# Batched x·yᵀ: stores of two heads in 16 KB runs with 64-column weight tiles, instead of four heads in 32 KB runs with 32-column tiles

## The chip, the cores and the metric

The kernel runs on one core of a Trainium2 chip. The metric is device time in microseconds, median of several executions. A trace of one core has a "span" from its first to its last instruction, here about 1.8 us shorter than the device time.

PE is the matrix engine and writes its results into a memory called PSUM; DVE and ACT copy them out of it, POOL casts inputs, and SP issues the DMAs. 16 DMA engines move the data, in packets; here a packet is one contiguous run of a partition (the 22 stores of before, 128 partitions each, are 2816 packets of 32 KB in the trace). PE gets a granted clock that varies: PEclk shows it in tenths of full speed, and "half clock" below is a 5 there (in the trace of before it is 1.00 up to 65 us, then mostly 0.50, and 0.634 in the mean). The page shows two queues of the kind "instruction"; one of their packets is called an "instruction fetch" below: 16 KB each on queue q8, 8 KB each on q14.

## The reference

```python
# x, y: (8, 12, 512, 64) float32; 96 heads of 512 rows
def reference(x, y):
    return np.einsum('bhtc,bhsc->bhts', x, y).astype(np.float32)
```

The inputs are 25 MB, the output is 101 MB. Each head is a 512 x 512 result with a contraction of 64.

## The kernel before

A group `g` is eight heads: `a` selects the half of the partitions that holds the contraction, and four heads lie beside each other in the columns. A partition of an output tile belongs to one head and holds 16 consecutive rows, 32 KB, which are contiguous in the output.

```python
P, G, Q, R, K = 128, 4, 32, 16, 8          # heads a tile, partitions a head, rows a partition, R/2
ov = out....rearrange("(g a p n) -> g a p n", a=2, p=P, n=R * S)
opool = tc.tile_pool(name="opool", bufs=3)  # output tiles of 32 KB a partition
# ... prepare(g): load, cast on POOL, transpose on PE, copy to xT and yT (half on DVE, half on ACT)
            dst = xT[:, half * K:(half + 1) * K]
            if half == 0:
                nc.vector.tensor_copy(dst, pt)
            else:
                nc.scalar.activation(dst, pt, COPY)
# ... main loop
        for a in range(2):
            ot = opool.tile([P, R, S], fp32)
            otf = ot.rearrange("p r s -> p (r s)")
            edge = (g == 0 and a == 0) or (g == NG - 1 and a == 1)
            for k in range(K):
                ...
                pm = pmpool.tile([P, 2, S], fp32)      # a PSUM tile
                for two in range(2):
                    for h in range(G):
                        nc.tensor.matmul(pm[h * Q:(h + 1) * Q, two, :],
                            xT[a * C:(a + 1) * C, 2 * k + two, h * Q:(h + 1) * Q],
                            yT[a * C:(a + 1) * C, h * S:(h + 1) * S], start=True, stop=True)
                # copy pm to ot[:, 2k:2k+2], on ACT for even k, on DVE for odd k
                if edge and k % 2 == 1:
                    i, j = (2 * k - 2) * S, (2 * k + 2) * S
                    nc.sync.dma_start(ov[g, a][:, i:j], otf[:, i:j])
            if not edge:
                nc.sync.dma_start(ov[g, a], otf)
```

Of the kernel before, what the change touches and what calls it, by code (L numbers as in the profile page):

```python
# [1 line left out]

# [5 lines left out]


@with_exitstack  # L10
def kernel(
    ctx: ExitStack,
    tc: tile.TileContext,
    x: bass.AP,
    y: bass.AP,
    out: bass.AP,
):





    nc = tc.nc
    B, H, T, C = x.shape
    _, _, S, _ = y.shape
    P = 128
    G = 4
    Q = P // G
    R = T // Q
    NG = B * H // (2 * G)  # L30
    K = R // 2
    AHEAD = 3
    fp32 = mybir.dt.float32
    bf16 = mybir.dt.bfloat16
    COPY = mybir.ActivationFunctionType.Copy
    assert C * 2 == P and S == T and R == 16

    xv = x.rearrange("b h t c -> (b h t c)").rearrange("(g a p n) -> g p a n", a=2, p=P, n=R * C)
    yv = y.rearrange("b h t c -> (b h t c)").rearrange("(g a p n) -> g p a n", a=2, p=P, n=R * C)
    ov = out.rearrange("b h t s -> (b h t s)").rearrange("(g a p n) -> g a p n", a=2, p=P, n=R * S)  # L40

    const = ctx.enter_context(tc.tile_pool(name="const", bufs=1))
    lpool = ctx.enter_context(tc.tile_pool(name="lpool", bufs=AHEAD))
    bpool = ctx.enter_context(tc.tile_pool(name="bpool", bufs=2))
    tpool = ctx.enter_context(tc.tile_pool(name="tpool", bufs=2))
    opool = ctx.enter_context(tc.tile_pool(name="opool", bufs=3))
    ptpool = ctx.enter_context(tc.tile_pool(name="ptpsum", bufs=2, space=bass.MemoryType.PSUM))
    pmpool = ctx.enter_context(tc.tile_pool(name="pmpsum", bufs=3, space=bass.MemoryType.PSUM))

    loaded = {}  # L50

    def load(g):
        xs = lpool.tile([P, 2, R, C], fp32)
        ys = lpool.tile([P, 2, R, C], fp32)
        nc.sync.dma_start(ys.rearrange("p a r c -> p a (r c)"), yv[g])  # L55
        nc.sync.dma_start(xs.rearrange("p a r c -> p a (r c)"), xv[g])
        loaded[g] = (xs, ys)

    for g in range(AHEAD):
        load(g)  # L60

    ident = const.tile([P, P], bf16)
    make_identity(nc, ident)

    def prepare(g, made):

        xs, ys = loaded.pop(g)
        yb = bpool.tile([P, R, 2, C], bf16)
        xb = bpool.tile([P, R, 2, C], bf16)
        for s, b in ((ys, yb), (xs, xb)):  # L70
            for half in range(2):
                rows = slice(half * K, (half + 1) * K)
                nc.gpsimd.tensor_copy(b[:, rows], s[:, :, rows].rearrange("p a r c -> p r a c"))  # L73
        if g + AHEAD < NG:
            load(g + AHEAD)
        yield
        yT = tpool.tile([P, G * Q, R], bf16)
        xT = tpool.tile([P, R, P], bf16)
        for half in range(2):
            pt = ptpool.tile([P, K, P], bf16)  # L80
            for k in range(K):
                nc.tensor.transpose(  # L82
                    pt[:, k, :], yb[:, half * K + k].rearrange("p a c -> p (a c)"), ident
                )
            dst = yT[:, :, half * K:(half + 1) * K]
            src = pt.rearrange("p k n -> p n k")
            if half == 0:
                nc.vector.tensor_copy(dst, src)  # L88
            else:
                nc.scalar.activation(dst, src, COPY)  # L90
            yield
        for half in range(2):
            pt = ptpool.tile([P, K, P], bf16)
            for k in range(K):
                nc.tensor.transpose(  # L95
                    pt[:, k, :], xb[:, half * K + k].rearrange("p a c -> p (a c)"), ident
                )
            dst = xT[:, half * K:(half + 1) * K]
            if half == 0:
                nc.vector.tensor_copy(dst, pt)  # L100
            else:
                nc.scalar.activation(dst, pt, COPY)  # L102
            yield
        made[g] = (xT, yT.rearrange("p n k -> p (n k)"))

    made = {}
    for _ in prepare(0, made):
        pass
    for g in range(NG):
        xT, yT = made.pop(g)  # L110
        steps = prepare(g + 1, made) if g + 1 < NG else iter(())
        for a in range(2):
            ot = opool.tile([P, R, S], fp32)
            otf = ot.rearrange("p r s -> p (r s)")
            edge = (g == 0 and a == 0) or (g == NG - 1 and a == 1)
            for k in range(K):
                if k in (0, 3, 6):
                    next(steps, None)
                pm = pmpool.tile([P, 2, S], fp32)
                for two in range(2):  # L120
                    for h in range(G):
                        nc.tensor.matmul(  # L122
                            pm[h * Q:(h + 1) * Q, two, :],
                            xT[a * C:(a + 1) * C, 2 * k + two, h * Q:(h + 1) * Q],
                            yT[a * C:(a + 1) * C, h * S:(h + 1) * S],
                            start=True, stop=True,
                        )
                if k % 2 == 0:
                    nc.scalar.activation(ot[:, 2 * k:2 * k + 2, :], pm, COPY)  # L129
                else:  # L130
                    nc.vector.tensor_copy(ot[:, 2 * k:2 * k + 2, :], pm)  # L131
                if edge and k % 2 == 1:
                    i, j = (2 * k - 2) * S, (2 * k + 2) * S
                    nc.sync.dma_start(ov[g, a][:, i:j], otf[:, i:j])
            if not edge:
                nc.sync.dma_start(ov[g, a], otf)  # L136


# [1 line left out]
_INS = ['x', 'y']  # L140
_OUTS = [((8, 12, 512, 512), 'float32')]


# [23 lines left out]
```

## Time and profile before

| | before |
|---|---|
| median time | 307.29 us (307.26 to 307.49) |
| span of the trace | 305.6 us |
| DMA data queue, share of 16 engines | 97.2% |
| PE, DVE, ACT busy | 67%, 45%, 39% |
| matmuls in all (with transposes) | 1920 |

The page of the kernel before. The slices are fortieths of the span, a digit is a busy share in tenths; the queue lines give packets, MB and share of 16 engines.

```profile
PE 203.8 (67%) x1920; PEld 91.5 (30%) x1920; DVE 138.4 (45%) x120; ACT 119.6 (39%) x121; POOL 49.3 (16%) x54
...
PEclk9999999975555555755675555575575555555555
DMA  7999999999999999999999999999999999999980
...
q1 hardware_dynamic: 10848, 125.83, 97.2%
q8 instruction: 15, 0.25, 0.3%
q14 instruction: 4, 0.03, 0.0%
...
L122 PE MATMUL pm<-yT,xT 64*32 64x512 bf16 x1536 | 159.4, 586 | 67.2 <-ACT ot L129 64.7
...
L100 DVE COPY xT<-pt 128x1024 bf16<-128x1024 bf16 x12 | 8.3, 690 | 12.3 <-PE pt L95 9.8
...
out_dram<-ot SPq DMA_DIRECT2D x22, 4096.0 KB, 27.4
```

DMA is at 9 from the second to the last but one busy slice: this kernel is bound by data movement (97.2% of 16 engines' span), and the compute engines wait for it (ACT 72.1 us and DVE 63.4 us for stores that still hold the output buffers). Then only two things can change the time by much: how long a DMA engine needs for its share, and how unevenly the 16 engines finish.

The trace also holds single packets and, for each DMA, the times of its 16 completions (one per DMA engine, as I read them: before each of the 16 of the last store a data packet ends, 0.43 us before it at most). In the packed trace a packet carries no engine number, but on an engine one packet begins where the one before it ends (within 20 ns in the chains followed), so an engine that is apart from the others can be followed. Sorted completions of the last store, as the distance behind the first of them:

```
kernel before, last store (us): first engine done at 295.86; then
+0.01 +0.18 +0.22 +0.71 +0.90 +0.93 +1.63 +2.60 +2.75 +2.82 +3.16 +3.28 +3.72 +4.66 +8.79
```

The other 15 engines have done their share by about 300.5 us, and the core waits four more microseconds for a single DMA engine. That one engine sets the end. Below it is called the drifting engine, because its lag grows from store to store.

The pace of the matmuls at half clock is read from an unbroken stretch in the timeline of before (start us, us, engine, line and what). 64 matmuls are eight PSUM tiles, so a tile takes 6.82 / 8 = 0.853 us. Within it, four matmuls start within 30 ns of each other, and the next four about 0.43 us after them: four run abreast.

```profile
266.39 6.82 PE L122 MATMUL pm<-yT,xT 64*32 64x512 bf16 x64 [3.19 <-ACT ot L129]
```

### The profile page before, as it was taken

To read this page: it belongs to the slowest core of one execution; us is meant where nothing else is said; L and a number is where in the kernel's file an instruction comes from. 1 tells how busy PE (TensorE), PEld (TensorE's weight loads), DVE (VectorE), ACT (ScalarE), POOL (GpSimd) and SP (SyncE) were. 2 spreads that over 40 slices of the span, in tenths; PEclk is the share of its full clock that TensorE was granted. 3 is DMA by queue.
4 is the path that set the end of the run, shared out by engine and by line. 5 is a ranking of instruction groups with operands and counts; after the bars stand their busy time and mean duration, and the time that the engine had idled before them with its cause. 6 is when DMAs were issued, how large, how long until landed. Compare 5 with 4: busy or idle time off the path is not lost.

```text
span 305.6 us, 4378 instructions
## 1 busy us (share of the span) xinstructions
PE 203.8 (67%) x1920; PEld 91.5 (30%) x1920; DVE 138.4 (45%) x120; ACT 119.6 (39%) x121; POOL 49.3 (16%) x54
## 2 busy tenths in 40 slices
PE   1899999969919928936932990991785976575000
PEld 1443234525404503512511540350251432222000
DVE  0465654657416507615633741670664664446000
ACT  1445527544523606505522451560653463325000
POOL 3755024300500500320140050041000000000000
PEclk9999999975555555755675555575575555555555
DMA  7999999999999999999999999999999999999980
GB/s 278 412 409 420 459 419 399 470 418 388 446 455 388 440 446 398 441 429 437 427 424 442 420 427 430 411 454 420 437 435 425 427 442 422 437 437 422 409 368 39
DMA packets 10867, 126.11 MB, mean 413 GB/s; under 512 B 864, under 2 KB 864, under 8 KB 7008
## 3 DMA queue, kind: packets, MB, share of 16 engines
q1 hardware_dynamic: 10848, 125.83, 97.2%
q8 instruction: 15, 0.25, 0.3%
q14 instruction: 4, 0.03, 0.0%
HBM read 25.17 MB, written 100.66 MB: 412 GB/s over the span
## 4 chain that ended last, share of the span: by engine, by line
DMA 49%; PE 29%; DVE 5%; issue 4%; ACT 3%; POOL 1%; SPq 0%; ACTq 0%
DMA out_dram<-ot 47%; PE pm L122 23%; DVE ot L131 5%; PE pt L95 4%; ACT ot L129 3%; PE pt L82 2%; DMA xs<-in_x_dram 2%; ACT xT L102 1%; POOL xb L73 1%; DVE xT L100 0%; SPq L55 0%; ACTq L129 0%; SPq L136 0%
## 5 line engine op out<-in xcount | busy, mean ns | idle before, releaser
L122 PE MATMUL pm<-yT,xT 64*32 64x512 bf16 x1536 | 159.4, 586 | 67.2 <-ACT ot L129 64.7
L131 DVE COPY ot<-pm 128x1024 f32<-128x1024 f32 x96 | 117.0, 1224 | 123.0 <-DMA out_dram<-ot 63.4
L129 ACT ACTIVATE ot<-pm 128x1024 f32<-128x1024 f32 x96 | 95.9, 1023 | 115.5 <-DMA out_dram<-ot 72.1
L122 PEld LDWEIGHTS <-xT 64*32 64x32 bf16 x1536 | 53.3, 118 | 148.1 <-issue 136.3
L73 POOL CAST yb<-ys 128x1024 bf16<-128x1024 f32 x24 | 24.3, 1040 | 143.5 <-PE pt L82 69.8
L82 PE MATMUL pt<-ident,yb 128*128 128x128 bf16 x192 | 23.9, 297 | 8.5 <-POOL yb L73 6.8
L102 ACT ACTIVATE xT<-pt 128x1024 bf16<-128x1024 bf16 x12 | 12.3, 1023 | 37.0 <-PE pt L95 30.3
L95 PE MATMUL pt<-ident,xb 128*128 128x128 bf16 x192 | 25.8, 310 | 1.3 <-DVE xT L100 0.8
L73 POOL CAST xb<-xs 128x1024 bf16<-128x1024 f32 x24 | 24.3, 1040 | 13.7 <-issue 4.9
L95 PEld LDWEIGHTS <-xb 128*128 128x128 bf16 x192 | 19.4, 143 | 22.7 <-issue 20.0
L82 PEld LDWEIGHTS <-yb 128*128 128x128 bf16 x192 | 19.3, 138 | 17.7 <-issue 8.2
L88 DVE COPY yT<-pt 128x1024 bf16<-128x1024 bf16 x12 | 14.6, 1216 | 8.5 <-PE pt L82 8.5
L90 ACT ACTIVATE yT<-pt 128x1024 bf16<-128x1024 bf16 x12 | 12.2, 1019 | 8.2 <-PE pt L82 8.2
L100 DVE COPY xT<-pt 128x1024 bf16<-128x1024 bf16 x12 | 8.3, 690 | 12.3 <-PE pt L95 9.8
L90 ACT ACT_TABLE_LOAD x1 | 1.3, 1283 | 0.7 <-PEq L151 0.7
masks.py:199 POOL TENSOR_SCALAR_AFFINE_SELECT ident<-ident 128x128 bf16<-128x128 bf16 x1 | 0.3, 292 | 0.1
masks.py:197 POOL MEMSET ident<- 128x128 bf16 x1 | 0.2, 204 | 0.3 <-POOLq L151 0.3
L151 POOL MEMSET const-float32-0.0<- 128x1 f32 x1 | 0.1, 98 | 0.2 <-issue 0.2
L151 POOL MEMSET const-bfloat16-1.0<- 128x1 bf16 x1 | 0.1, 101 | 0.0
L151 POOL MEMSET const-uint8-127<- 128x1 uint8 x1 | 0.1, 101 | 0.0
L151 POOL MEMSET const-float32-1.0<- 128x1 f32 x1 | 0.1, 98 | 0.0
## 6 DMA issues: line engine op xcount, KB each, us to landing
out_dram<-ot SPq DMA_DIRECT2D x22, 4096.0 KB, 27.4
ys<-in_y_dram SPq DMA_DIRECT2D x12, 1024.0 KB, 21.2
xs<-in_x_dram SPq DMA_DIRECT2D x12, 1024.0 KB, 23.4
out_dram<-ot SPq DMA_DIRECT2D x8, 1024.0 KB, 19.2
```

The source lines that it names most:

```text
L73: nc.gpsimd.tensor_copy(b[:, rows], s[:, :, rows].rearrange("p a r c -> p r a c"))
L82: nc.tensor.transpose(pt[:, k, :], yb[:, half * K + k].rearrange("p a c -> p (a c)"), ident)
L88: nc.vector.tensor_copy(dst, src)
L90: nc.scalar.activation(dst, src, COPY)
L95: nc.tensor.transpose(pt[:, k, :], xb[:, half * K + k].rearrange("p a c -> p (a c)"), ident)
L100: nc.vector.tensor_copy(dst, pt)
L102: nc.scalar.activation(dst, pt, COPY)
L122: nc.tensor.matmul(pm[h * Q:(h + 1) * Q, two, :], xT[a * C:(a + 1) * C, 2 * k + two, h * Q:(h + 1) * Q], yT[a * C:(a + 1) * C, h * S:(h + ...
L129: nc.scalar.activation(ot[:, 2 * k:2 * k + 2, :], pm, COPY)
L131: nc.vector.tensor_copy(ot[:, 2 * k:2 * k + 2, :], pm)
L151: nc = _bacc.Bacc("TRN2", target_bir_lowering=False, num_devices=1)
```

## The change

The output tile is halved: two heads of 64 partitions each, eight rows a partition, 16 KB. A weight tile then has 64 columns instead of 32, so half as many matmuls do the same work. For this the 64 columns of a head must be its 32 row blocks with both halves of eight rows, and the copy into `xT` interleaves them. There are 44 stores of 2 MB instead of 22 of 4 MB, and six buffers of half the size. Loads, casts and `y` stay as they are.

```diff
-    ov = ....rearrange("(g a p n) -> g a p n", a=2, p=P, n=R * S)
+    ov = ....rearrange("(g a p n) -> g a p n", a=4, p=P, n=K * S)
-    opool = ...(name="opool", bufs=3)
+    opool = ...(name="opool", bufs=6)
-        xT = tpool.tile([P, R, P], bf16)
+        xT = tpool.tile([P, K, P, 2], bf16)
 ...
-            dst = xT[:, half * K:(half + 1) * K]
+            dst = xT[:, half * K // 2:(half + 1) * K // 2]
+            src = pt.rearrange("p (e i) n -> p i n e", e=2)
 ...
+            for pair in range(2):
+                ot = opool.tile([P, K, S], fp32)
 ...
-                    for h in range(G):
-                        nc.tensor.matmul(pm[h * Q:(h + 1) * Q, two, :],
-                            xT[a * C:(a + 1) * C, 2 * k + two, h * Q:(h + 1) * Q],
-                            yT[a * C:(a + 1) * C, h * S:(h + 1) * S], ...)
+                        for h in range(2):
+                            col = (2 * pair + h) * Q
+                            nc.tensor.matmul(pm[h * 64:(h + 1) * 64, two, :],
+                                xT[a * C:(a + 1) * C, 2 * k + two, col:col + Q].rearrange("c n e -> c (n e)"),
+                                yT[a * C:(a + 1) * C, (2 * pair + h) * S:(2 * pair + h + 1) * S], ...)
 ...
-                nc.sync.dma_start(ov[g, a], otf)
+                    nc.sync.dma_start(ov[g, 2 * a + pair], otf)
```

More of the change, by code (lines that the diff above doesn't have):

```diff
@@ L39 @@
     yv = y.rearrange("b h t c -> (b h t c)").rearrange("(g a p n) -> g p a n", a=2, p=P, n=R * C)
-    ov = out.rearrange("b h t s -> (b h t s)").rearrange("(g a p n) -> g a p n", a=2, p=P, n=R * S)
+    ov = out.rearrange("b h t s -> (b h t s)").rearrange("(g a p n) -> g a p n", a=4, p=P, n=K * S)
     const = ctx.enter_context(tc.tile_pool(name="const", bufs=1))
@@ L45 @@
     tpool = ctx.enter_context(tc.tile_pool(name="tpool", bufs=2))
-    opool = ctx.enter_context(tc.tile_pool(name="opool", bufs=3))
+    opool = ctx.enter_context(tc.tile_pool(name="opool", bufs=6))
     ptpool = ctx.enter_context(tc.tile_pool(name="ptpsum", bufs=2, space=bass.MemoryType.PSUM))
@@ L94, in prepare @@
             for k in range(K):
+                e, i = divmod(k, K // 2)
                 nc.tensor.transpose(
-                    pt[:, k, :], xb[:, half * K + k].rearrange("p a c -> p (a c)"), ident
+                    pt[:, k, :], xb[:, e * K + half * K // 2 + i].rearrange("p a c -> p (a c)"), ident
                 )
-            dst = xT[:, half * K:(half + 1) * K]
+            dst = xT[:, half * K // 2:(half + 1) * K // 2]
+            src = pt.rearrange("p (e i) n -> p i n e", e=2)
             if half == 0:
-                nc.vector.tensor_copy(dst, pt)
+                nc.vector.tensor_copy(dst, src)
             else:
-                nc.scalar.activation(dst, pt, COPY)
+                nc.scalar.activation(dst, src, COPY)
             yield
@@ L112 @@
         for a in range(2):
-            ot = opool.tile([P, R, S], fp32)
-            otf = ot.rearrange("p r s -> p (r s)")
-            edge = (g == 0 and a == 0) or (g == NG - 1 and a == 1)
-            for k in range(K):
-                if k in (0, 3, 6):
-                    next(steps, None)
-                pm = pmpool.tile([P, 2, S], fp32)
-                for two in range(2):
-                    for h in range(G):
-                        nc.tensor.matmul(
-                            pm[h * Q:(h + 1) * Q, two, :],
-                            xT[a * C:(a + 1) * C, 2 * k + two, h * Q:(h + 1) * Q],
-                            yT[a * C:(a + 1) * C, h * S:(h + 1) * S],
-                            start=True, stop=True,
-                        )
-                if k % 2 == 0:
-                    nc.scalar.activation(ot[:, 2 * k:2 * k + 2, :], pm, COPY)
-                else:
-                    nc.vector.tensor_copy(ot[:, 2 * k:2 * k + 2, :], pm)
-                if edge and k % 2 == 1:
-                    i, j = (2 * k - 2) * S, (2 * k + 2) * S
-                    nc.sync.dma_start(ov[g, a][:, i:j], otf[:, i:j])
@@ L135 @@
-            if not edge:
-                nc.sync.dma_start(ov[g, a], otf)
+            for pair in range(2):
+                ot = opool.tile([P, K, S], fp32)
+                otf = ot.rearrange("p r s -> p (r s)")
+                edge = (g == 0 and a == 0) or (g == NG - 1 and a == 1)
+                for k in range(K // 2):
+                    if (pair * K // 2 + k) in (0, 3, 6):
+                        next(steps, None)
+                    pm = pmpool.tile([P, 2, S], fp32)
+                    for two in range(2):
+                        for h in range(2):
+                            col = (2 * pair + h) * Q
+                            nc.tensor.matmul(
+                                pm[h * 64:(h + 1) * 64, two, :],
+                                xT[a * C:(a + 1) * C, 2 * k + two, col:col + Q].rearrange("c n e -> c (n e)"),
+                                yT[a * C:(a + 1) * C, (2 * pair + h) * S:(2 * pair + h + 1) * S],
+                                start=True, stop=True,
+                            )
+                    if k % 2 == 0:
+                        nc.scalar.activation(ot[:, 2 * k:2 * k + 2, :], pm, COPY)
+                    else:
+                        nc.vector.tensor_copy(ot[:, 2 * k:2 * k + 2, :], pm)
+                    if edge and k % 2 == 1:
+                        i, j = (2 * k - 2) * S, (2 * k + 2) * S
+                        nc.sync.dma_start(ov[g, 2 * a + pair][:, i:j], otf[:, i:j])
+                if not edge:
+                    nc.sync.dma_start(ov[g, 2 * a + pair], otf)
```

## The prediction

Three passages are cut from the prediction and marked. Its sum came to 307.3 + 0.9 - 3.6, about 304.7 us. Its 9 fetches can be had from the page of before, as an estimate: 15 for 3840 matmuls and weight loads make 9.0 for 2304. Its 27.2 GB/s and 0.04 us can be had from the two times beside them: 192 KB more take 7.23 us, which is 27.2 GB/s, and at that pace the 256 KB of 9.68 us take 9.64. That two 64-column matmuls run abreast was an estimate, for a case that no run had shown yet.

> **What bounds the kernel now.** The DMA engines. The page's slices show DMA at 9 in all but the first and last two slices; the queue table gives 97.2% of 16 engines' span. PE is busy 67%, DVE 45%, ACT 39%. The table by stretches gives 429 to 433 GB/s from 100 to 280 us, at a granted clock near 0.5, so the half clock costs nothing. The long pieces of the chain of waits are stores (22 to 34 us): compute waits for output buffers.
>
> **What sets the end.** The trace's packets are regular: loads 159 ns for 4 KB, stores 309 ns for 8 KB and 1213 ns for 32 KB, back to back. But the 16 completions of the last store come from 295.9 to 304.6 us: the median engine is 1.6 us behind the first, the second to last 4.7, the last 8.8. Two causes show:
> - The instruction queue fetched 15 pieces of 16 KB (PE has 3842 instructions[...]). After each, one engine is about 1.6 us later, mostly a different one.
> - One engine drifts steadily to 8.8 us, without a fetch. Its 32 KB packets take 52 to 89 ns longer while compute runs, nothing while it is idle or after 281 us. The excess comes in steps of about 4.7 ns, roughly one per matmul, DVE, ACT or POOL record ending during the packet (12 matmuls and 1 to 3 others: 61 to 71 ns). 1920 matmuls and some 300 others give about 10 us (estimate), near 8.8. I can't name the mechanism, only the proportion.
>
> **What the change does.**
> - Stores: 22 of 4 MB become 44 of 2 MB, 16 KB a packet; the 8 small ones stay. On the first engine 4 MB take 9.68 us (eight packets), 1 MB 2.45 us; at 27.2 GB/s per engine both leave about 0.04 us per eight packets with completion. Extra: 22 x 0.04 = 0.9 us on each engine. [...]
> - Matmuls: 1536 of 32 columns become 768 of 64. Before, seven PSUM tiles took 5.97 us at half clock, 0.853 us each, eight matmuls four abreast. After, four matmuls two abreast: also 0.853 us. [...]
> - PE instructions fall to 2306: 9 fetches. 768 fewer matmuls take 768 x 4.7 ns = 3.6 us from the drifting engine.
> - DVE copies of xT get a strided source: 690 to about 1216 ns (as yT now), 12 times, 6 us on an engine 45% busy: nothing. ACT stays near 1020 ns. Six half-size buffers: the queues were never empty, so nothing.
>
> **Sum.** 307.3 + 0.9 - 3.6 = about 304.7 us, faster by 0.9%. Range 302.8 to 307.6. Faster by over 2% 0.04, within 2% 0.92, slower 0.04.
>
> **What would show it.** 16 KB packets of about 611 ns; 9 fetches; last completions about 5 us apart; DVE xT near 1216 ns; 0.85 us per PSUM tile at half clock; first engine done 0.9 us later.
>
> **What would make it wrong.** If two 64-column tiles don't run abreast, PE needs 1.7 us per tile, 328 us in all: slower by over 6%. If the drift doesn't follow the matmul count, about 308.2. If a fetch falls on the drifting engine, 1.6 us later. If 16 KB runs go worse at HBM, slower.

## The result, and the profile after

| | before | after |
|---|---|---|
| median time | 307.39 us (307.26 to 307.75) | 306.30 us (305.95 to 306.72) |
| ratio | | 0.9963, 95% interval 0.9946 to 0.9981 |
| span of the trace | 305.6 us | 304.3 us |
| first engine done with the last store | 295.86 us | 296.63 us |
| last engine done with it | 304.64 us (+8.79) | 303.21 us (+6.57) |

A ratio is the mean time of one kernel's runs over that of the other's of the same rounds, so it is not quite the ratio of the medians quoted. The gain is real, but it is 1.1 us and not the 2.7 us predicted, though the predicted time was only 1.6 us off.

The page of the changed kernel, the lines that answer to those of before:

```profile
PE 208.5 (69%) x1152; PEld 104.6 (34%) x1152; DVE 144.7 (48%) x120; ACT 119.4 (39%) x121; POOL 49.3 (16%) x54
...
PEclk9999999999999855555555655555555555555555
DMA  7999999999999999999999999999999999999992
...
q1 hardware_dynamic: 14016, 125.83, 98.2%
q8 instruction: 9, 0.15, 0.2%
...
L126 PE MATMUL pm<-yT,xT 64*64 64x512 bf16 x768 | 164.0, 610 | 56.0 <-ACT ot L133 53.9
...
L102 DVE COPY xT<-pt 128x1024 bf16<-128x1024 bf16 x12 | 14.7, 1223 | 10.8 <-PE pt L96 9.4
...
out_dram<-ot SPq DMA_DIRECT2D x44, 2048.0 KB, 28.3
```

And the timeline of after, in a stretch at half clock; 32 matmuls are again eight PSUM tiles:

```profile
242.48 6.91 PE L126 MATMUL pm<-yT,xT 64*64 64x512 bf16 x32 [2.03 <-ACT ot L133]
```

That is 0.864 us a tile, within about 1% of before: two 64-column tiles run abreast as four 32-column ones did (two matmuls start within 55 ns, the next two about 0.43 us after them). The instruction queue fetched 9 pieces instead of 15. The strided copy to `xT` on DVE went from 690 to 1223 ns and cost nothing that can be seen (experiment 3 below has it, experiment 2 has not, and they are 0.1 us apart). DMA stays at 9 throughout. All this is as predicted. The completions of the last store are not:

```
kernel after, last store (us): first engine done at 296.63; then
+0.10 +0.13 +0.37 +0.81 +0.83 +1.47 +1.48 +1.49 +1.55 +1.78 +2.53 +3.13 +4.10 +6.49 +6.57
```

The last engine is 6.57 us behind, not about 5, and a second one stands right beside it. Followed packet by packet, the last one is not the drifting engine: that one is at 6.49, and the one at 6.57 was thrown back by an instruction fetch (see the last bullet under "Why the prediction was wrong").

### The profile page after: what moved, and what is told of

Read it like the earlier page. It is cut to its first block, busy times and chain, and to the rows that moved or that the text cites. A ratio compares the mean times of both kernels' runs of the same rounds, so it can differ in the third digit from the quotient of the medians.

```text
span 304.3 us, 2968 instructions
## 1 busy us (share of the span) xinstructions
PE 208.5 (69%) x1152; PEld 104.6 (34%) x1152; DVE 144.7 (48%) x120; ACT 119.4 (39%) x121; POOL 49.3 (16%) x54
## 4 chain that ended last, share of the span: by engine, by line
DMA 60%; PE 23%; DVE 4%; ACT 2%; issue 1%; POOL 1%; SPq 0%; ACTq 0%
DMA out_dram<-ot 48%; PE pm L126 17%; DMA xs<-in_x_dram 12%; PE pt L82 3%; PE pt L96 3%; DVE ot L135 2%; ACT ot L133 2%; DVE xT L102 1%; POOL xb L73 1%; SPq L55 0%; ACTq L133 0%; SPq L140 0%; ACT xT L104 0%; SPq L56 0%
## 5 line engine op out<-in xcount | busy, mean ns | idle before, releaser
L126 PE MATMUL pm<-yT,xT 64*64 64x512 bf16 x768 | 164.0, 610 | 56.0 <-ACT ot L133 53.9
L135 DVE COPY ot<-pm 128x1024 f32<-128x1024 f32 x96 | 117.2, 1223 | 113.3 <-PE pm L126 57.3
L126 PEld LDWEIGHTS <-xT 64*64 64x64 bf16 x768 | 66.1, 150 | 131.2 <-issue 122.7
L96 PE MATMUL pt<-ident,xb 128*128 128x128 bf16 x192 | 24.9, 310 | 1.1 <-POOL xb L73 0.9
L102 DVE COPY xT<-pt 128x1024 bf16<-128x1024 bf16 x12 | 14.7, 1223 | 10.8 <-PE pt L96 9.4
```

What stands on the lines that cost most here:

```text
L96: nc.tensor.transpose(pt[:, k, :], xb[:, e * K + half * K // 2 + i].rearrange("p a c -> p (a c)"), ident)
L102: nc.vector.tensor_copy(dst, src)
L126: nc.tensor.matmul(pm[h * 64:(h + 1) * 64, two, :], xT[a * C:(a + 1) * C, 2 * k + two, col:col + Q].rearrange("c n e -> c (n e)"), yT[a * ...
L135: nc.vector.tensor_copy(ot[:, 2 * k:2 * k + 2, :], pm)
```

## The experiments

The theory: the end is that of the slowest DMA engine. One engine is delayed a little by every instruction that the compute engines finish (an instruction's end, as the trace records it, is called a record below), so fewer matmuls help; smaller packets cost all DMA engines something, and that takes part of the gain away. The main rival: the gain comes from the finer stores and buffers, which keep the DMA queues better filled. In all experiments, "lag" is the distance of the last completion of the last store behind the first one.

### 1. The matmul half alone

```diff
 # the kernel before
-                    for h in range(G):
-                        matmul(pm[h*Q:(h+1)*Q, two, :], xT[..., h*Q:(h+1)*Q], yT[..., h*S:(h+1)*S])
+                    for h in range(2):
+                        matmul(pm[h*64:(h+1)*64, two, :], xT[..., h*64:(h+1)*64], yT[..., 2*h*S:(2*h+1)*S])
```

Half of the values are wrong: two heads share one head's `y`.

> The kernel before with 64-column weights, half the matmuls (768 instead of 1536), stores unchanged at 4 MB in 32 KB packets; half the results are wrong on purpose. Theory (the last DMA engine is delayed by about 4.7 ns per matmul): last engine's lag falls from 8.8 to 5 to 6.5 us, first engine ends as before, time about 305.3 us, that is lower than the changed kernel by its 0.8 us of store cost. Rival (smaller stores and finer buffers made the gain): no gain here, 307.4 us.

Measured: 304.47 us (304.44 to 304.50), ratio 0.9904 (0.9889 to 0.9919). First engine done at 295.82 us, as before; lag 5.91. The matmul half alone gives 2.9 us, more than the whole change. The rival falls: stores and buffers were untouched.

Half as many matmuls also bring half as many weight loads and only 9 fetches. That the gain is not one of the fetches shows in the packets. Summed over all 32 KB packets, what they took beyond 1213 ns (those over 250 ns, which come with a fetch, left out) was 7.6 us before and 4.8 us here, 2.8 us less. (Such sums are rough: for 16 KB packets the changed kernel has 5.2 us and experiment 4, of the same time, 3.9.)

### 2. The store half alone

```diff
 # the kernel before, 32-column matmuls kept
-    opool = ...(name="opool", bufs=3)
+    opool = ...(name="opool", bufs=6)
 ...
+                if k % 4 == 0:
+                    ot = opool.tile([P, K, S], fp32)
 ...
-            if not edge:
-                nc.sync.dma_start(ov[g, a], otf)
+                if not edge and k % 4 == 3:
+                    nc.sync.dma_start(ov[g, a][:, base:base + K * S], otf)   # base = (k // 4) * K * S
```

> The kernel before with its 32-column matmuls, but stores of 2 MB in 16 KB packets from six half-size buffers. Theory: first engine ends 0.8 us later, lag of the last engine stays near 8.8 us, time about 308.2 us. Rival (finer buffers made the gain): about 306.3 us, as the changed kernel.

Measured: 308.89 us (308.77 to 308.98), ratio 1.0047 (1.0031 to 1.0064). First engine done at 296.74, 0.88 later; lag 9.29. So the stores cost 1.5 us, not 0.9: 0.9 on every engine, and the last one falls behind by a further 0.5. With the first experiment, the change is taken apart completely:

| medians, us | 1536 matmuls of 32 columns | 768 of 64 columns | effect of the matmuls |
|---|---|---|---|
| 32 KB packets | 307.41 (before) | 304.47 (1) | -2.9 |
| 16 KB packets | 308.89 (2) | 306.30 (after) | -2.6 |
| effect of the packets | +1.5 | +1.8 | |

The page of experiment 1 and that of experiment 2, the DMA queue and the matmuls: each has one half of the change.

```profile
q1 hardware_dynamic: 10848, 125.83, 98.1%
q8 instruction: 9, 0.15, 0.2%
...
L122 PE MATMUL pm<-yT,xT 64*64 64x512 bf16 x768 | 158.8, 585 | 65.3 <-ACT ot L129 62.6
```

```profile
q1 hardware_dynamic: 14016, 125.83, 97.4%
q8 instruction: 15, 0.25, 0.3%
...
L124 PE MATMUL pm<-yT,xT 64*32 64x512 bf16 x1536 | 157.5, 583 | 66.6 <-ACT ot L131 61.0
```

PE is busy for 158.8 and 157.5 us in these groups. Half as many matmuls save no PE time at all, yet nearly 3 us of the kernel's time.

### 3. The matmuls put back, another way

```diff
 # the changed kernel
+                            for s0 in range(0, S, 256):
-                                pm[h*64:(h+1)*64, two, :], xT[...], yT[..., head]
+                                pm[h*64:(h+1)*64, two, s0:s0+256], xT[...], yT[..., head, s0:s0+256]
```

> The changed kernel with each matmul of 512 columns cut into two of 256: 1536 matmuls again, 15 instruction fetches again, same stores, PE array time about the same. Theory: last engine's lag back near 8.8 us, time 308.2 us or a bit more. Rival (the number of matmuls does not matter, stores do): 306.3 us.

Measured: 308.97 us (308.88 to 309.00), lag 9.28. The result equals that of experiment 2 within 0.1 us: with small stores it is the number of PE instructions that counts, not the width of the weight tile.

### 4. Packets against DMAs

```diff
 # the changed kernel
-    opool = ...(name="opool", bufs=6)
+    opool = ...(name="opool", bufs=3)
+            big = opool.tile([P, 2, K, S], fp32)      # ot = big[:, pair]
 ...
-                    nc.sync.dma_start(ov[g, 2 * a + pair], otf)
+            nc.sync.dma_start(ov[g, 2*a:2*a+2].rearrange("a p n -> p a n"), big as [P, 2, K*S])
```

> The changed kernel, but the two 2 MB tiles of an a go out in one 4 MB store of 16 KB packets: 30 DMAs instead of 52, buffers of 32 KB again. If the 0.8 us of the first engine is the cost of a packet, it stays (306.3 us); if it is the cost of a DMA and its completion, the first engine ends about 0.6 us earlier (305.6 us). Rival (finer buffers made the gain): 307.4 us.

Measured: 306.24 us (305.94 to 306.48), ratio 0.9961; the first engine at 296.72, lag 6.66. So neither the number of DMAs and completions nor the finer buffers matter; the cost is one of each packet.

### 5 and 6. Instructions that have nothing to do with PE

```diff
 # the kernel before; experiment 6 has nc.gpsimd in place of nc.vector
+                for i in range(4):
+                    nc.vector.memset(scratch[:, i:i + 1], 0.0)
                 pm = pmpool.tile([P, 2, S], fp32)
```

> The kernel before with four tiny DVE memsets of an unused scratch tile ahead of each PSUM tile, 768 in all; PE and stores unchanged. If any engine's instruction records delay the last DMA engine as matmuls do (3.7 ns each, as 768 fewer matmuls gave 2.8 us): lag of the last engine 8.8 + 2.8 = 11.6 us, time 310.2 us. If it is something of the matmul alone (its weight loads, its instruction fetches or PSUM writes): 307.4 us.

> The same with the 768 tiny memsets on POOL. If every record counts alike: 310.2 us. The fit over single packets gave DVE 3.7 to 5.3 ns a record and POOL about 0, so by that fit POOL adds nothing: 307.4 us.

Measured: with DVE 309.42 us (309.36 to 309.47), lag 10.90; with POOL 308.87 us (308.75 to 308.96), lag 10.34. Both are dearer than before, though PE and the stores are as before, so it is nothing of the matmul alone. My fit that gave POOL nothing was wrong. Both are below the 2.8 us that 768 records should add. The scheduler let these memsets run ahead, all before about 80 us, partly while nothing but loads was in flight; and they bring six more instruction fetches of 8 KB (10 instead of 4), so the totals are not clean. Single packets are. This is the q14 line of the page of experiment 5, and from its timeline one stretch in which DVE ran a burst of memsets.

```profile
q14 instruction: 10, 0.08, 0.1%
...
70.96 4.07 DVE L121 MEMSET scratch<- 128x1 f32 x129
```

And these are 32 KB packets that took longer than the usual 1213 ns, with the number of instruction records that ended meanwhile:

```
kernel         start us  longer by  DVE  ACT  POOL  matmul
before           116.22      52 ns    0    1     0      12
before           167.41      66 ns    1    0     0      12
before           190.57      14 ns    1    1     0       4
experiment 5      44.58     221 ns   46    5     2      10
experiment 5      72.52     155 ns   44    0     0       0
experiment 5      73.89     174 ns   44    0     0       0
experiment 6      54.36     178 ns    1    0    36      14
experiment 6      57.15     174 ns    1    1    35      10
```

In the fifth and sixth row PE did nothing: 44 DVE records lengthen one packet by 155 to 174 ns, 3.5 to 4 ns each. POOL records do the same (36 of them with 15 others: 178 ns, 3.5 ns each). Weight loads are not counted in the table: in its third row eleven of them ended too, and the packet took only 14 ns longer with six other records, so a weight load adds nothing that can be seen.

### 7. Fewer bytes for one DMA engine at the end

```diff
 # the kernel before, its last two 1 MB stores
-                    nc.sync.dma_start(ov[g, a][:, i:j], otf[:, i:j])
+                    nc.sync.dma_start(ov[g, a][0:120, i:j], otf[0:120, i:j])
+                    nc.sync.dma_start(ov[g, a][120:128, i:j], otf[120:128, i:j])
```

The idea was that a store of 120 partitions leaves one DMA engine without data, and that this could be the slow one. Which engine is left out was my assumption, which no trace or run shows; two clauses with it are cut from the expectation and marked. "It" is the engine that ends last: first for the case that it is the one left out, and so rid of two 1 MB stores of 2.45 us.

> The kernel before, but its last two 1 MB stores are each cut into 120 partitions and 8 partitions[...]. [...]it is rid of 4.9 us and the others get about 0.35 us more: the last completion moves from 8.8 us behind to about 5, time 303.5 to 304 us. If it is another engine, time rises by about 0.35 us, to 307.8 us. If the end isn't set by one engine but by the sum of the DMA work: 307.4 us.

Measured: 311.16 us (309.56 to 311.27), ratio 1.0111. A miss, and dearer than any of the three expectations. The trace, of the run of 309.56 us, bears out the number of engines: of the 16 completions of a 120-partition store, one comes when it is issued and 15 come with the data; of an 8-partition store, 8 come with the data. It doesn't show which engines these are. The slow engine was not relieved: the completions of the 120-partition stores still have one engine about 10 us behind the first of them. The last completion of each 8-partition store follows 0.3 us behind it (304.15 after 303.84, 306.92 after 306.60), so the slow engine is one of the eight that carry both stores, and it got the added 8 KB packets instead of being rid of anything. These packets are 0.6 us in all; in the trace another 1.4 us of lag came on the slow engine in the 1 MB store ahead of the split ones. Why, and why the other three runs took 311.1 to 311.3 us, was not found out.

### 8. Fewer matmuls still

```diff
 # the kernel before
-                    for h in range(G): matmul(pm[h*Q:(h+1)*Q, two, :], xT[..., h*Q:(h+1)*Q], yT[..., head h])
+                    matmul(pm[:, two, :], xT[..., :], yT[..., head 0])
```

Wrong: all four heads get one head's `y`.

> The kernel before with 128-column weights: 384 matmuls instead of 1536, one head's values in all four heads, wrong on purpose; stores of 4 MB in 32 KB packets. By 3.7 ns a matmul the slow engine falls another 1.4 us below that with 64 columns (lag 5.9): lag 4.5 us, 303.0 us, unless an engine delayed by instruction fetches comes last by then. If the second run of fetches sets the end (4 to 5 us behind), it stops near 303.5 us.

Measured: 303.18 us (303.05 to 303.25), lag 4.31. Another 384 matmuls fewer give another 1.3 us, 3.4 ns each.

### 9 and 10. Smaller packets still, and both together with right results

Experiment 9 is experiment 2 with quarter tiles:

```diff
 # the kernel before
-    opool = ...(name="opool", bufs=3)
+    opool = ...(name="opool", bufs=12)
+                if k % 2 == 0:
+                    ot = opool.tile([P, 4, S], fp32)
 ...
+                if k % 2 == 1:
+                    nc.sync.dma_start(ov[g, a][:, base:base + 4 * S], otf)   # base = (k // 2) * 4 * S
```

Experiment 10 interleaves four row blocks instead of two, so that one head fills 128 columns:

```diff
 # experiment 10, from the changed kernel
-        xT = tpool.tile([P, K, P, 2], bf16)
+        xT = tpool.tile([P, 4, P, 4], bf16)
-            src = pt.rearrange("p (e i) n -> p i n e", e=2)
+            src = pt.rearrange("p (j i) n -> p i n j", j=4)
 ...
+                        nc.tensor.matmul(pm[:, two, :], xT[..., r + two, hd*Q:(hd+1)*Q] as 128 columns, yT[..., head hd])
 ...
+                    nc.sync.dma_start(ov[g, two heads].rearrange("h p n -> p h n"), ot)   # 8 KB runs
```

> The kernel before with its 32-column matmuls, all stores in 1 MB pieces of 8 KB packets from twelve quarter-size buffers: 528 more packets on each DMA engine than before (16 KB packets were 176 more, and cost 1.5 us in all, 0.9 us of it on the first engine). If the cost is one of each packet: first engine 2.6 us later, last engine 4.5 us later, time 311.9 us. If it came of the 2 MB size or the DMA count, something else; if finer buffers help, under 308.9 us.

> The same trade one step further, with right results: 384 matmuls of 128 columns, stores of one head a row block in 8 KB packets, 2 MB each. From the 128-column kernel with 32 KB packets (303.2 us) plus 528 packets (4.5 us): 307.7 us, so worse than the changed kernel (306.3). If only the first engine's cost counts (2.6 us): 305.8 us, and it beats both.

Measured: experiment 9 takes 312.56 us (312.12 to 312.84), first engine at 299.86, lag 10.30. Experiment 10 is correct and takes 309.15 us (309.02 to 309.40), first engine at 300.31, lag 6.19. 528 more packets on each engine cost 5.2 us over before (9.8 ns a packet) and 6.0 us over experiment 8 (11 ns a packet). The first engine of experiment 9 is 4.0 us later than before, not 2.6. (All four executions of experiment 9 had a granted clock of 1.0, those of before 0.63 to 0.68; experiment 10, at 0.61 to 0.65, shows a like cost, so the clock is not its cause.) So the packet cost holds in kind and is somewhat more than expected, and going further in the change's direction loses. Of the right kernels tried, the changed one and experiment 4 are the fastest, and they are equal.

### 11. The converse, spread over the kernel

```diff
 # the kernel before, behind each DVE copy out of PSUM
+                    for i in range(8):
+                        nc.vector.tensor_copy(scratch[:, i:i + 1], ot[:, 2 * k, i:i + 1])
```

> The kernel before with 768 one-element DVE copies, eight behind each DVE copy out of PSUM, so that they run through the whole kernel. In single packets 44 DVE records without any PE work cost 155 to 174 ns, 3.5 to 4 ns a record. So last engine's lag 8.8 + 2.7 to 3.1 us, time 310.1 to 310.5 us, the converse of the change's 768 fewer matmuls. If records only count by the instruction fetches they bring (6 of 8 KB, 0.3 us each, on several engines): under 308.5 us.

Measured: 309.59 us (309.40 to 309.72), ratio 1.0071, lag 11.27, first engine at 295.71. The lag rose by 2.5 us, 3.2 ns for each added copy, a little less than expected; the time is well above the bound of 308.5 us that the expectation set for fetches alone, and the 32 KB packets' sum (see experiment 1) rose from 7.6 to 10.1 us. The groups of this run show the added work: small, and on an engine with time to spare (DVE is busy 61% of the span).

```profile
L134 DVE COPY scratch<-ot 128x1 f32<-128x1 f32 x768 | 52.8, 144 | 1.4
```

## Why the prediction was wrong

- **What bounds the kernel: right.** It is the DMA engines: the PE groups of experiments 1 and 2 are busy for about equally long (158.8 and 157.5 us) and the times differ by 4.4 us, and the coarse buffers of 4 change nothing.
- **What sets the end, one slow DMA engine that is delayed by each finished instruction: right in kind for the kernel before.** Experiments 1, 3, 8 and 11 move its lag down and up with the number of instructions, and 5 and 6 show in single packets that DVE and POOL records count as matmuls do. "Without a fetch" was not quite so: at 186.3 us an 8 KB fetch of 309 ns fell between two packets of this engine, and the packet behind it took 274 ns longer.
- **Matmuls at the same pace, 9 fetches, 611 ns packets, DVE copies at 1223 ns: right.**
- **"768 x 4.7 ns = 3.6 us": mis-sized.** Measured 2.9 us with large stores (experiment 1) and 2.6 us with small ones (after against 2): 3.4 to 3.8 ns a matmul. 4.7 ns is the step in which single packets lengthen; I took the step for the mean. The same trace had the better figure: 8.8 us of lag over the some 2220 records that I counted (all but the weight loads) is 4.0 ns each, 3.7 without that one fetch, and the prediction saw "about 10" against 8.8 and passed over it. With 3.4 to 3.8 ns this term alone is 0.7 to 1.0 us too large.
- **"22 x 0.04 = 0.9 us": mis-sized, in the other direction.** Measured 1.5 us (2 against before) and 1.8 us (after against 1). I had read the cost off the first engine to finish, and there it held: 0.8 to 0.9 us later. But the end is set by the last engine, which fell back 0.5 to 0.7 us more. For each of the 176 packets added on an engine the last engine's cost is 8 to 10 ns, the first one's about 5. The packets' own durations come near it, 2 x 611 - 1213 = 9 ns for each added packet, times 22 x 8 packets an engine, is 1.6 us; but they are the same on the first engine, which lost half of that. Why the last engine loses more stays open.
- **"Last completions about 5 us apart": wrong, 6.57.** Besides the two sizes, the engine that ends last is another one. The drifting engine ended at 6.49. A second engine, which with the fetches had come to 5.3 us behind, went to 6.7 between two neighbouring stores, at the time of the ninth large instruction fetch (265.6 us; one of its packets took 364 ns longer), and ended at 6.57; before, the second to last had been at 4.66. So part of the path was wrong too: in the changed kernel a fetch-delayed engine ends last, though only 0.08 us behind the drifting one. Experiment 4 shows the same (5.3 to 6.8 us at the fetch of 270.7 us, last at 6.66, the drifting engine at 6.59). I had looked for a fetch on the drifting engine and not for one on an engine already far behind. How much of the 0.8 us of spread among the changed kernel's four runs is due to this stays open; experiment 1, with as many fetches, had its second engine at 4.25 and times within 0.06 us.

The sum with measured terms: -2.6 or -2.9 for the matmuls and +1.5 or +1.8 for the packets, -1.1 us either way, which is the result.

What is not shown is how a finished instruction reaches a DMA engine. What is measured is that the instructions of PE, DVE and POOL count, at 3 to 4 ns each, on one DMA engine (3.4 to 3.8 ns a matmul; in single packets 3.5 to 4 ns a DVE record and 3.5 ns where most were POOL's), and that weight loads, which the trace records too, add nothing that can be seen. By what mechanism stays open. All executions here were recorded, so no run tells whether an unrecorded one has the same slow engine, and thus whether the matmul half of the gain would be there.

## What to carry to other kernels

In a kernel bound by DMA, look at when each of the 16 DMA engines completes the last store, not only at the mean busy share: four microseconds of this one were one engine alone, and once that lag shrinks, another engine may be the last (here at 6.57 us, the drifting one at 6.49). Take the cost of a change from the engine that ends last, and use mean costs over the whole trace rather than the step of a single event. Before you judge a gain of a few tenths of a per cent from fewer, larger instructions, ask whether it comes from the instructions' work or from their number: here PE's groups were busy for as long (159.4 us before, 158.8 in experiment 1), and the time fell by 2.9 us. Whether it would fall in an execution that is not recorded, no run here tells.
